# The later modulation's loads moved from SP's queue to GpSimd's, with five tiles instead of three in the second half

## The chip, the cores and the metric

The kernel runs on one core of a Trainium2 chip. The metric is the device time of one execution in microseconds (us). TensorE (PE) multiplies matrices, VectorE (DVE) and ScalarE (ACT) work element by element, GpSimd (POOL) does little here, and SyncE (SP) issues nearly all transfers (DMAs). Each engine works its own instructions off in order and waits for others through semaphores. A DMA is issued by an instruction on some engine's queue, and that instruction may itself wait first.

## What is computed

A decoder trunk of two layers over one sequence of 512 positions and 2048 features, in float32. Layer 0 is differential attention with a SiLU gate, layer 1 forgetting attention over keys and values that are projected once between the two. Ahead of each layer the input is modulated by vectors that come from a condition `c`:

```python
c_act = silu(c)                                   # one row of 2048
for l in range(2):
    shift, scale, gate = split(c_act @ w_mod[l] + b_mod[l], 3)
    h = x * (1 + scale) + shift
    if l == 0:
        y = diff_attention(h, a_w_in, a_w_out, ...)
    else:
        kshift, kscale = split(c_act @ kv_w_mod + kv_b_mod, 2)
        k, v, F = shared_kv(x * (1 + kscale) + kshift, kv_w, kv_b_f)
        y = forgetting_attention(h, b_w_in, b_w_out, k, v, F)
    x = layer_norm(ALPHA * x + gate * y)
```

The products `c_act @ w_mod[l]` and `c_act @ kv_w_mod` are one row times a matrix. Those matrices are large all the same: `w_mod` has 2 x 2048 x 6144 elements and `kv_w_mod` 2048 x 4096.

## The kernel before

**The big products.** Each float32 operand is split into a high part, rounded to the `fp32r` form, and a low part, and a product is three matmuls (`products`, lines 173 to 175). Weights come in steps of 256 rows by 512 columns (`WeightStream`): SP loads a step into a tile `wst` (line 46, four tiles), ScalarE rounds it to `whi` (line 93) and VectorE subtracts to get `wlo` (line 94), three tiles of each. One step feeds 24 matmuls of 512 columns. `group` runs eight such steps for 512 output columns; after every sixth of a step's matmuls (a burst of six) it calls `tick`, which runs one queued piece (attention, for instance) and, where `bg` says so, one step of the background.

**The background: the later modulation.** The shift and scale of layer 0 are made at the start, in another way (`sms`, line 449). All later modulation rows are made by `mod_stream` on VectorE, beside the big products. A segment is 512 columns of one such row: sixteen tiles of 128 rows by 512 columns are multiplied by the matching elements of `c_act` and added into one tile `macc` (line 384 the first of a segment, line 386 the others). Here each such multiply-add is called just that. The summed tile is then split (`mhi`, `mlo`), summed over partitions by two matmuls with a matrix of ones (lines 406 and 407), the bias row `mrow` (loaded at line 403) is added at line 408, and the row goes to DRAM (line 409, tensors `mod_dram` and `gate_dram`), where a later step reads it. There is one `mrow`, so the next bias load waits for the row before to be stored.

There are two such streams.

- The first runs during layer 0: 16 segments, tiles `ms` of two row blocks (512 KB, two multiply-adds), two tiles, one load ahead.
- The second runs during the shared keys and values: 8 segments, tiles `ms` of one row block (256 KB, one multiply-add), three tiles, two loads ahead. The forget gate's rows (`head_rows`) share these tiles.

A load of `ms` (line 369) is issued on SP's queue and waits until the multiply-adds that used the tile are done.

**What sets the order.** The program is written in the order of the big products with `tick` between. A scheduler then fixes each engine's order when the kernel is built, by its own estimate of times: a multiply-add depends on no matmul, so it may be put well ahead of the place where `tick` asks for it, as far as its tiles allow. VectorE's order of multiply-adds and `wlo` subtractions is thus decided when the kernel is built, and at run time a multiply-add whose tile hasn't landed holds up everything behind it on VectorE.

**Attention.** In the first stream's time VectorE also normalises attention outputs (`og`, line 753), which TensorE transposes soon after (line 767).

Of the kernel before, what the change touches and what calls it, by code (L numbers as in the profile page):

```python
# [9 lines left out]
F32 = mybir.dt.float32  # L10
# [5 lines left out]
P = 128  # L16
# [93 lines left out]
def tile_yoco(  # L110
# [23 lines left out]
    nc = tc.nc  # L134
    V, S, PE, G = nc.vector, nc.scalar, nc.tensor, nc.gpsimd
# [25 lines left out]
    def tr_bank(name="tr"):  # L161
        return ps.tile([P, 512], F32, name=name, tag="tr", bufs=1)

    def o_bank(name="o"):
        return ps.tile([P, 512], F32, name=name, tag="o", bufs=1)

    def split(hi, lo, src):
        S.copy(hi, src)
        V.tensor_tensor(lo, src, hi.bitcast(F32), op=ALU.subtract)
# [48 lines left out]
    rows = {}  # L218
# [136 lines left out]
    def mod_stream(segs, new_stage, new_acc, nk):  # L355


        todo = [(i, r) for i in range(len(segs)) for r in range(KT // nk)]
        loaded = {}
        summed = []  # L360

        def load(k):
            if k >= len(todo):
                return
            i, r = todo[k]
            src, col, _ = segs[i]
            t = new_stage()
            rows = src[nk * r * P : nk * (r + 1) * P, col : col + 512]
            nc.sync.dma_start(t, rows.rearrange("(k p) n -> p k n", p=P) if nk > 1 else rows)
            loaded[k] = t  # L370

        ahead = 2 // nk
        for k in range(ahead):
            load(k)
        for k, (i, r) in enumerate(todo):
            load(k + ahead)
            if r == 0:
                acc = new_acc()
            t = loaded.pop(k)
            for kk in range(nk):  # L380
                kt = nk * r + kk
                w = t[:, kk, :] if nk > 1 else t
                if kt == 0:
                    V.tensor_scalar(acc, w, cact[:, 0:1], None, op0=ALU.mult)
                else:
                    V.scalar_tensor_tensor(acc, w, cact[:, kt : kt + 1], acc, op0=ALU.mult, op1=ALU.add)  # L386
                if kt == KT - 1:
                    summed.append(segs[i][2](acc))
                if kt in (1, 5) and summed:
                    if next(summed[0], None) is None:  # L390
                        summed.pop()
                yield
        for _ in summed[0]:
            yield

    def mod_row(pool, ones_r, dst, bias, one):

        def steps(acc):
            hi = pool.tile([P, 512], F32R, name="mhi", tag="mhi", bufs=1)
            lo = pool.tile([P, 512], F32R, name="mlo", tag="mlo", bufs=1)  # L400
            split(hi, lo, acc)
            row = pool.tile([1, 512], F32, name="mrow", tag="mrow", bufs=1)
            nc.sync.dma_start(row, bias.rearrange("(o n) -> o n", o=1))
            yield True
            pt = tr_bank()
            PE.matmul(pt, ones_r, hi, start=True, stop=False)
            PE.matmul(pt, ones_r, lo, start=False, stop=True)
            V.scalar_tensor_tensor(row, pt[0:1, :], one, row, op0=ALU.add, op1=ALU.add)
            nc.sync.dma_start(dst, row)
        return steps  # L410


# [4 lines left out]
    with tc.tile_pool(name="start", bufs=2, reuse_waits="tile") as sp, tc.manual_schedule(engines={ET.DVE}):  # L417
# [64 lines left out]
        ahead = [next(steps)]  # L482
# [147 lines left out]
    for dst, src, col, bias, one in (  # L630
# [5 lines left out]
        for f0 in range(0, D, 512):  # L636
            cs = slice(col + f0, col + f0 + 512)
            segs.append((src, col + f0, mod_row(ap, ones_a, dst[:, f0 : f0 + 512], bias[cs], one)))
    background = mod_stream(
        segs,  # L640
        lambda: ap.tile([P, 2, 512], F32, name="ms", tag="ms", bufs=2),
# [313 lines left out]
    npool, n, nstats = zp  # L955
# [37 lines left out]
    fz = {}  # L993

    def head_rows(tag, bufs):
        return npool.tile([P, T], F32, name="rows", tag=tag, bufs=bufs)[0:B_HEADS, :]

    def forget_logits(q):
        def fn():
            if q == 0:  # L1000
                fz["ps"] = o_bank("zfp")
            for kt in range(4 * q, 4 * q + 4):
                w = zp64[:, kt : kt + 2, :].rearrange("p k n -> p (k n)")
                PE.matmul(fz["ps"], w, Hh[kt], start=kt == 0, stop=False)
                PE.matmul(fz["ps"], w, Hl[kt], start=False, stop=kt == KT - 1)
            if q == 3:
                fz["z"] = head_rows("ms", 3)
                V.tensor_scalar(fz["z"], fz["ps"][0:B_HEADS, :], bf, None, op0=ALU.add)
                V.tensor_tensor(fz["z"], fz["ps"][32 : 32 + B_HEADS, :], fz["z"], op=ALU.add)
        return fn  # L1010

    def forget_sums():

        zf = fz["z"]
        e, w, ln = head_rows("ms", 3), head_rows("ms", 3), head_rows("macc", 2)
        V.scalar_tensor_tensor(e, zf, -1.0, zf, op0=ALU.mult, op1=ALU.max)
        S.activation(e, e, AF.Exp, scale=-1.0)
        V.tensor_scalar(w, e, 1.0, None, op0=ALU.add)
        S.activation(ln, w, AF.Ln)

        V.scalar_tensor_tensor(e, w, -1.0, e, op0=ALU.add, op1=ALU.subtract)
        V.reciprocal(w, w)
        V.tensor_tensor(e, e, w, op=ALU.mult)
        V.tensor_tensor(ln, ln, e, op=ALU.subtract)
        V.scalar_tensor_tensor(zf, zf, 0.0, ln, op0=ALU.min, op1=ALU.subtract)
        V.memset(w, 1.0)
        fz["nf"] = head_rows("macc", 2)
        V.tensor_tensor_scan(fz["nf"], w, zf, 0.0, op0=ALU.mult, op1=ALU.subtract)
        nc.sync.dma_start(f_dram, fz["nf"])
# [29 lines left out]
    for dst, col, one in ((mod_dram[1][1:2, :], D, 1.0), (gate_dram[1], 2 * D, 0.0)):  # L1059
        for f0 in range(0, D, 512):  # L1060
            cs = slice(col + f0, col + f0 + 512)
            segs.append((w_mod[1], col + f0, mod_row(npool, ones_b, dst[:, f0 : f0 + 512], b_mod[1, cs], one)))
    background = mod_stream(
        segs,
        lambda: npool.tile([P, 512], F32, name="ms", tag="ms", bufs=3),
        lambda: npool.tile([P, 512], F32, name="macc", tag="macc", bufs=2),
        1,
    )
# [230 lines left out]
```

## Time and profile before

| What | us |
|---|---|
| Median of 3 runs | 2016.16 (2014.56 to 2017.47) |
| The profiled execution | 2017.03 |
| Its span, from the first to the last instruction | 2015.2 |
| VectorE busy in the span | 1334.4 |
| ScalarE busy in the span | 722.3 |

In the profile's rows, `ms` loads read `in_w_mod_dram` or `in_kv_w_mod_dram`. The first stream's multiply-adds lie between about 186 and 840 us of the span, the second stream's between about 1095 and 1319 us. In a group's row, the number behind `x` is the count, then come the busy time in us and the mean of one in ns, then the idle time just before such instructions and what ended most of it. In a row of waits stand the waiting engine, tile and line, what it waited for, and then the sum in us, how often, and the longest. "SPq" is the time of an issuing instruction on SP.

### The profile page before, as it was taken

The page shows a single profiled execution, that of the slowest core. Times are in us where ns is not written, and L with a number is a line of the kernel's source. Part 1 is how long each engine was busy: PE and PEld are TensorE (multiplying, and loading weights), DVE is VectorE, ACT ScalarE, POOL GpSimd, SP SyncE. Part 2 cuts the span into 40 slices and gives each one's busy share as a digit, 9 for nine tenths or more (in the row PEclk, how much of TensorE's full clock was granted, in tenths as well). Part 3 has the DMA queues.
Part 4 walks back from the last instruction along what each step waited for, and adds up shares of the span by engine and source line. Part 5 has one row for each costly group of instructions (what it writes and reads, how often), then busy time and mean ns, then how long its engine had stood idle before and what let it go on. Part 6 is the DMA issues. An engine that isn't in the chain of part 4 may idle for free.

```text
span 2015.2 us, 25053 instructions
## 1 busy us (share of the span) xinstructions
PE 1966.7 (98%) x9115; PEld 1624.6 (81%) x9115; DVE 1334.4 (66%) x2435; ACT 722.3 (36%) x1230; POOL 2.2 (0%) x10
## 2 busy tenths in 40 slices
PE   5999999999999999999999999999999999999997
PEld 4888878888878888888878877888888888888885
DVE  7887878777667677753575666645455555576678
ACT  2423444433333334432273222224333333453232
POOL 0000000000000000000000000000000000000000
PEclk8999999999999999999999999999999999999998
DMA  9995755574556565552344878844233323333754
GB/s 342 346 314 149 238 174 162 166 222 156 190 166 210 160 225 178 162 165 94 115 144 135 268 252 260 259 123 129 90 104 95 104 90 104 95 117 93 259 191 177
DMA packets 263095, 353.79 MB, mean 176 GB/s; under 512 B 18022, under 2 KB 162556, under 8 KB 262204
## 3 DMA queue, kind: packets, MB, share of 16 engines
q1 hardware_dynamic: 260592, 347.99, 53.7%
q10 hardware_dynamic: 2380, 4.21, 0.6%
q8 instruction: 71, 1.16, 0.2%
q14 instruction: 52, 0.43, 0.1%
HBM read 339.47 MB, written 12.66 MB: 175 GB/s over the span
## 4 chain that ended last, share of the span: by engine, by line
PE 77%; DVE 10%; DMA 10%; issue 2%; ACT 1%; SPq 1%; DVEq 0%; ACTq 0%
PE acc L173 22%; PE acc L175 22%; PE acc L174 22%; DMA ms<-in_w_mod_dram 7%; DVE macc L386 3%; DVE wlo L94 2%; PE sc L173 2%; PE sc L174 2%; PE sc L175 1%; DMA ms<-in_kv_w_mod_dram 1%; PE o L175 1%; PE o L174 1%; PE o L173 1%; PE tr L1163 1%; DMA sms<-in_w_mod_dram 1%
## 5 line engine op out<-in xcount | busy, mean ns | idle before, releaser
L93 ACT CAST whi<-wst 128x1024 fp32r<-128x1024 f32 (+2 forms) x339 | 349.5, 1032 | 672.9 <-PE acc L175 281.6
L94 DVE TENSOR_TENSOR wlo<-wst,whi 128x1024 fp32r<-128x1024 f32 (+2 forms) x339 | 404.4, 1195 | 268.1 <-ACT whi L93 263.9
L173 PE MATMUL acc<-whi,hh 128*128 128x512 f32 x1252 | 492.6, 397 | 0.9 <-ACT hh L933 0.8
L174 PE MATMUL acc<-wlo,hh 128*128 128x512 f32 x1252 | 489.7, 391 | 2.6 <-DVE wlo L94 2.6
L175 PE MATMUL acc<-whi,hl 128*128 128x512 f32 x1252 | 488.1, 390 | 0.0
L173 PE MATMUL acc<-hh,whi 128*128 128x512 f32 x1184 | 468.5, 396 | 1.3 <-ACT vt L977 0.9
L175 PE MATMUL acc<-hh,wlo 128*128 128x512 f32 x1184 | 462.3, 390 | 2.0 <-DVE wlo L94 2.0
L174 PE MATMUL acc<-hl,whi 128*128 128x512 f32 x1184 | 461.7, 390 | 0.0
L386 DVE SCALAR_TENSOR_TENSOR macc<-ms,cact,macc 128x512 f32<-128x512 f32 x360 | 269.9, 750 | 128.4 <-DMA ms<-in_w_mod_dram 95.6
L175 PEld LDWEIGHTS acc<-whi,hl 128*128 128x128 f32 x1252 | 235.3, 188 | 50.8 <-DVE hl L934 0.3
L174 PEld LDWEIGHTS acc<-wlo,hh 128*128 128x128 f32 x1252 | 235.6, 188 | 47.8 <-DVE wlo L94 4.3
L173 PEld LDWEIGHTS acc<-whi,hh 128*128 128x128 f32 x1252 | 235.7, 188 | 46.8 <-ACT hh L933 1.2
L175 PEld LDWEIGHTS acc<-hh,wlo 128*128 128x128 f32 x1184 | 222.3, 188 | 52.2 <-DVE wlo L94 4.2
L173 PEld LDWEIGHTS acc<-hh,whi 128*128 128x128 f32 x1184 | 222.5, 188 | 45.7 <-ACT vt L977 1.7
L174 PEld LDWEIGHTS acc<-hl,whi 128*128 128x128 f32 x1184 | 222.6, 188 | 41.1
L476 DVE SCALAR_TENSOR_TENSOR sacc<-sms,cact,sacc 128x512 f32<-128x512 f32 (+1 forms) x127 | 89.5, 705 | 4.8 <-DMA sms<-in_w_mod_dram 1.2
L1152 ACT ACTIVATE eb<-eb,mnb 128x128 f32<-128x128 f32 (+1 forms) x64 | 36.1, 563 | 96.4 <-DVE mnb L1149 95.2
L703 ACT ACTIVATE e<-e,mn 128x128 f32<-128x128 f32 (+3 forms) x64 | 36.0, 563 | 89.5 <-DVE mn L699 88.7
L1149 DVE CUSTOM_DVE_ANT_0 eb<-sc,biasb 128x128 f32<-128x128 f32 (+1 forms) x64 | 31.3, 490 | 52.7 <-PE sc L175 52.7
L1167 DVE TENSOR_TENSOR pTl<-tr,pTh 128x128 fp32r<-128x128 f32 (+1 forms) x64 | 31.2, 487 | 26.5 <-ACT pTh L1166 26.2
L1166 ACT CAST pTh<-tr 128x128 fp32r<-128x128 f32 (+1 forms) x64 | 27.2, 424 | 43.6 <-PE tr L1163 43.1
L769 ACT ACTIVATE ogT<-tr,subg 128x128 f32<-128x128 f32 x64 | 20.0, 364 | 56.4 <-PE tr L767 56.4
(251 smaller groups left out, 1739.2 us busy)
## 6 DMA issues: line engine op xcount, KB each, us to landing
wst<-in_a_w_in_dram SPq DMA_DIRECT2D x240, 256.0 KB
ms<-in_w_mod_dram SPq DMA_DIRECT2D x64, 512.0 KB
ms<-in_kv_w_mod_dram SPq DMA_DIRECT2D x64, 512.0 KB
wst<-in_kv_w_dram SPq DMA_DIRECT2D x64, 512.0 KB
ms<-in_w_mod_dram SPq DMA_DIRECT2D x128, 256.0 KB
wst<-in_b_w_in_dram SPq DMA_DIRECT2D x128, 256.0 KB
sms<-in_w_mod_dram SPq DMA_DIRECT2D x56, 512.0 KB
wst<-in_b_w_out_dram SPq DMA_DIRECT2D x48, 512.0 KB
```

The lines of the kernel that those rows point to most:

```text
L93: self.nc.scalar.copy(hi[:, :, :w], st[:, :, :w])
L94: self.nc.vector.tensor_tensor(lo[:, :, :w], st[:, :, :w], hi[:, :, :w].bitcast(F32), op=ALU.subtract)
L173: PE.matmul(dst, lhs[0], rhs[0], start=start, stop=False)
L174: PE.matmul(dst, lhs[0], rhs[1], start=False, stop=False)
L175: PE.matmul(dst, lhs[1], rhs[0], start=False, stop=stop)
L386: V.scalar_tensor_tensor(acc, w, cact[:, kt : kt + 1], acc, op0=ALU.mult, op1=ALU.add)
L476: V.scalar_tensor_tensor(acc, w, sc, acc, op0=ALU.mult, op1=ALU.add)
L703: S.activation(e[:, :w], e[:, :w], AF.Exp, bias=mn, scale=-1.0, accum_out=rs)
L1149: V.tensor_tensor_reduce(out=e[:, :w], in0=sc[:, :w], in1=bias[:, :w], scale=-1.0, scalar=3.0e38, op0=ALU.add, op1=ALU.min, accum_out=mn)
L1152: S.activation(e[:, :w], e[:, :w], AF.Exp, bias=mn, scale=-1.0, accum_out=rs)
L1166: S.copy(pTh[:, 0 : i + 1, ts], src)
L1167: V.tensor_tensor(pTl[:, 0 : i + 1, ts], src, pTh[:, 0 : i + 1, ts].bitcast(F32), op=ALU.subtract)
```

## The change

Three edits:

- The loads of `ms`, the bias loads and the stores of finished rows (lines 369, 403, 409) are issued on GpSimd's queue instead of SP's. This holds for both streams.
- The second stream has five `ms` tiles instead of three, and loads four ahead instead of two. The first stream keeps two tiles and one ahead.
- The forget gate's rows, which share the second stream's tiles, ask for the same five.

```diff
             rows = src[nk * r * P : nk * (r + 1) * P, col : col + 512]
-            nc.sync.dma_start(t, rows.rearrange("(k p) n -> p k n", p=P) if nk > 1 else rows)
+            G.dma_start(t, rows.rearrange("(k p) n -> p k n", p=P) if nk > 1 else rows)
             loaded[k] = t

-        ahead = 2 // nk
+        ahead = 4 if nk == 1 else 1
...
             row = pool.tile([1, 512], F32, name="mrow", tag="mrow", bufs=1)
-            nc.sync.dma_start(row, bias.rearrange("(o n) -> o n", o=1))
+            G.dma_start(row, bias.rearrange("(o n) -> o n", o=1))
...
-            nc.sync.dma_start(dst, row)
+            G.dma_start(dst, row)
...
-                fz["z"] = head_rows("ms", 3)
+                fz["z"] = head_rows("ms", 5)
...
-        e, w, ln = head_rows("ms", 3), head_rows("ms", 3), head_rows("macc", 2)
+        e, w, ln = head_rows("ms", 5), head_rows("ms", 5), head_rows("macc", 2)
...
-        lambda: npool.tile([P, 512], F32, name="ms", tag="ms", bufs=3),
+        lambda: npool.tile([P, 512], F32, name="ms", tag="ms", bufs=5),
```

The change also moves instructions. Two places show it. The first is VectorE where the second stream begins, in the second value group of the shared keys and values; `L1028` is the end of the forget gate, `x4` means four in a row. Before:

```order
L1028 SCALAR_TENSOR_TENSOR rows<-rows 16x512
L384 TENSOR_SCALAR macc<-ms,cact 128x512
L1035 TENSOR_SCALAR F<-tr 128x64
L94 TENSOR_TENSOR wlo<-wst,whi 128x1024
L386 SCALAR_TENSOR_TENSOR macc<-ms,cact,macc 128x512 x4
L94 TENSOR_TENSOR wlo<-wst,whi 128x1024
L386 SCALAR_TENSOR_TENSOR macc<-ms,cact,macc 128x512 x3
L94 TENSOR_TENSOR wlo<-wst,whi 128x1024
L386 SCALAR_TENSOR_TENSOR macc<-ms,cact,macc 128x512 x4
L94 TENSOR_TENSOR wlo<-wst,whi 128x1024
```

The same place of VectorE's order now:

```order
L1028 SCALAR_TENSOR_TENSOR rows<-rows 16x512
L384 TENSOR_SCALAR macc<-ms,cact 128x512
L386 SCALAR_TENSOR_TENSOR macc<-ms,cact,macc 128x512
L1035 TENSOR_SCALAR F<-tr 128x64
L386 SCALAR_TENSOR_TENSOR macc<-ms,cact,macc 128x512 x2
L94 TENSOR_TENSOR wlo<-wst,whi 128x1024
L386 SCALAR_TENSOR_TENSOR macc<-ms,cact,macc 128x512 x6
L94 TENSOR_TENSOR wlo<-wst,whi 128x1024
L386 SCALAR_TENSOR_TENSOR macc<-ms,cact,macc 128x512 x5
L94 TENSOR_TENSOR wlo<-wst,whi 128x1024
```

Where three or four multiply-adds stood between two `wlo`, five to seven stand now. The first ten steps behind this place's first `wlo` hold 58 multiply-adds instead of 35; from the twelfth step on, bursts of sixteen in three steps take turns with three or four steps that hold none. Over the whole stream the number is the same, 128.

The second place is SP's queue at the same point of the program (`L1029` stores the forget gate's sums), before:

```order
L46 DMA wst<-in_kv_w_dram 128x2x512
L1029 DMA f_dram<-rows 16x512
L369 DMA ms<-in_w_mod_dram 128x512 x3
L46 DMA wst<-in_kv_w_dram 128x2x512
L369 DMA ms<-in_w_mod_dram 128x512 x4
L46 DMA wst<-in_kv_w_dram 128x2x512
```

And now, on SP:

```order
L46 DMA wst<-in_kv_w_dram 128x2x512 x11
L1029 DMA f_dram<-rows 16x512
L46 DMA wst<-in_kv_w_dram 128x2x512 x25
L898 DMA mrow_b<-mod_dram_76 32x128
L46 DMA wst<-in_kv_w_dram 128x2x512 x21
```

And the start of the second stream on GpSimd, which has nothing else to do there:

```order
L403 DMA mrow<-in_b_mod_dram 1x16x32
L369 DMA ms<-in_w_mod_dram 128x512 x43
L409 DMA mod_dram_76<-mrow 16x1x32
L369 DMA ms<-in_w_mod_dram 128x512
L403 DMA mrow<-in_b_mod_dram 1x16x32
L369 DMA ms<-in_w_mod_dram 128x512 x25
```

SP is left with the weights, and the modulation's loads, bias rows and stores follow one another on GpSimd in the order of the stream.

## The prediction

> **What bounds the kernel now.** I read the busy shares and slices first, then the chain's shares.
>
> ```profile
> PE 1966.7 (98%) x9115; PEld 1624.6 (81%) x9115; DVE 1334.4 (66%) x2435; ACT 722.3 (36%) x1230; POOL 2.2 (0%) x10
> ...
> PE   5999999999999999999999999999999999999997
> ...
> PEclk8999999999999999999999999999999999999998
> DMA  9995755574556565552344878844233323333754
> ...
> PE 77%; DVE 10%; DMA 10%; issue 2%; ACT 1%; SPq 1%; DVEq 0%; ACTq 0%
> ```
>
> TensorE sets the time, at a full granted clock from slice 2 on, and GpSimd stands idle. The windows then say how much TensorE loses, and where (columns: window and its length, busy time and instructions of each engine, clock, DMA share, GB/s).
>
> ```profile
> 0.00:50.00 50.00, 29.04 (x129) 23.42 (x130) 35.51 (x65) 11.78 (x15) 1.60 (x9) 0.90 1.02 342
> 186.00:840.00 654.00, 647.47 (x3050) 536.61 (x3048) 477.11 (x988) 253.77 (x512) 0.00 (x0) 1.00 0.60 188
> 900.00:1000.00 100.00, 100.00 (x443) 82.84 (x442) 42.27 (x61) 20.65 (x22) 0.00 (x0) 1.00 0.33 103
> 1095.00:1319.00 224.00, 218.81 (x954) 177.25 (x953) 144.36 (x182) 55.91 (x66) 0.00 (x0) 1.00 0.78 253
> 2000.00:2016.00 16.00, 1.54 (x7) 0.94 (x5) 11.23 (x22) 0.00 (x0) 0.00 (x0) 0.65 0.32 131
> ```
>
> The first and last rows hold idle time that the change can't reach. The changed loads run in the second row (256 multiply-adds, first modulation stream) and the fourth (128, second stream). From 900 to 1000 us, 443 matmuls pass in 100 us, so one per 0.2257 us. At that pace the fourth window had room for 992 matmuls and holds 954: 38 are missing, **8.6 us lost**. In the second window 654.0 - 647.5 = **6.5 us** are idle. So 15 us is the most that better loads can give back. What TensorE waited for there, the second stream's window first, then the first's:
>
> ```profile
> PE acc L174 <- DVE wlo L94: 2.3, 3, 1.0
> PE acc L175 <- DVE wlo L94: 2.0, 4, 0.9
> ```
> ```profile
> PE tr L767 <- DVE og L753: 4.4, 5, 1.3
> ```
>
> Both are VectorE results that come late. And what VectorE waited for, the second stream's window first:
>
> ```profile
> DVE macc L386 <- DMA ms<-in_w_mod_dram: 72.5, 49, 3.6
> ```
> ```profile
> DVE wlo L94 <- ACT whi L93: 56.9, 36, 4.2
> DVE macc L386 <- DMA ms<-in_kv_w_mod_dram: 26.8, 27, 2.9
> DVE macc L386 <- DMA ms<-in_w_mod_dram: 23.1, 23, 3.1
> DVE macc L384 <- DMA ms<-in_w_mod_dram: 3.1, 2, 2.0
> ```
>
> VectorE works in order: a multiply-add that waits for its `ms` tile holds up the `wlo` (or `og`) behind it. What counts is how long a load takes from a tile's release to its landing, and how the order mixes the two kinds of work.
>
> **The change, part by part.**
>
> *SP relieved.* 256 loads and 48 small transfers leave SP's queue. That is worth nothing by itself: ScalarE, which takes the weights first, waits for TensorE to free its buffers in the second stream (first row), and in the whole first stream only 4.9 us for weights (second).
>
> ```profile
> ACT whi L93 <- PE acc L174: 49.4, 14, 5.6
> ```
> ```profile
> ACT whi L93 <- DMA wst<-in_a_w_in_dram: 4.9, 2, 4.4
> ```
>
> *The second stream, before.* From the `wlo` at 1099.70 to that at 1247.83 VectorE makes 24 weight steps. The grouped rows count what lies between.
>
> ```profile
> 1099.70 1.22 DVE L94 TENSOR_TENSOR wlo<-wst,whi 128x1024 fp32r<-128x1024 f32 x1 [2.49 <-ACT whi L93]
> ...
> 1247.83 1.22 DVE L94 TENSOR_TENSOR wlo<-wst,whi 128x1024 fp32r<-128x1024 f32 x1
> ```
> ```profile
> L386 DVE SCALAR_TENSOR_TENSOR macc<-ms,cact,macc 128x512 f32<-128x512 f32 x80 | 60.0, 751 | 54.6 <-DMA ms<-in_w_mod_dram 53.3
> L94 DVE TENSOR_TENSOR wlo<-wst,whi 128x1024 fp32r<-128x1024 f32 x25 | 30.4, 1217 | 2.5 <-ACT whi L93 2.5
> ...
> L384 DVE TENSOR_SCALAR macc<-ms,cact 128x512 f32<-128x512 f32 x5 | 2.4, 482 | 0.2 <-DMA ms<-in_w_mod_dram 0.2
> ```
>
> TensorE needs 24 matmuls, 5.42 us, per step: 130.1 us. VectorE took 148.1, so it fell 18.0 us behind. TensorE lost 8.6 of that; the other **9.4 us** were its lead (three `whi`/`wlo` buffers). The 85 multiply-adds went at 148.1/85 = 1.74 us each. The load time comes from the chain of waits, which has 23 `ms` rows between 1096 and 1262 us: the shortest, one near the middle, and the longest.
>
> ```profile
> 1155.96 3.99 DMA ms<-in_w_mod_dram
> ...
> 1232.13 2.82 DMA ms<-in_w_mod_dram
> ...
> 1120.66 6.13 DMA ms<-in_w_mod_dram
> ```
>
> The chain follows what came last, so I take 4.0 for a typical load L, just under the middle of 4.35. Three tiles go round in L plus one multiply-add: (4.0 + 0.75)/3 = 1.58 us. The remaining 0.16 is what `wlo` and the other small work add.
>
> *The second stream, after.* Five tiles alone make it (4.75 + d)/5 + 0.16 = 1.11 + 0.2d us per multiply-add, where d is what the new queue and the fuller pipe add to L. But the order has also changed, and that is the trap: the rows now put 58 multiply-adds into the ten steps after the first `wlo` instead of 35. TensorE gives ten steps 54.2 us plus 9.4 of lead, 63.6. VectorE needs 58 x (1.11 + 0.2d) = 64.4 + 11.6d. The loss is 0.8 + 11.6d in place of 8.6: a **net of -7.8 + 11.6d**. Later bursts of 16 in three steps stand behind three or four bare steps, and five tiles are ready, so they cost nothing up to about d = 2. One bias transfer now waits ahead of loads on GpSimd in the dense stretch, for the previous row's store to land: up to one load time, hidden by four tiles in hand. The forget gate's rows share the five tiles, so two loads can start before those rows are done; that is worth one wait at the stretch's start, and I count nothing.
>
> *What d is.* The trace has no load issued from GpSimd. From below: a load from the emptier queue might land as the fastest row did, d = 2.82 - 4.0 = -1.2. From above: the slowest row, d = 6.13 - 4.0 = +2.1. I take **d = 1.0**: two more tiles in flight are 0.52 MB, 1.5 us at the 342 GB/s of the first window, and with the DMA engines 0.78 busy most of that queues. This is nearer to the upper row, and it asks nothing yet of GpSimd's own work. Net: +3.8 us.
>
> The Trainium skill, page "DMA: Bandwidth & Descriptors", section "Latency and other measured facts", gives the first byte as about 0.6 us after an issue from SP and 1 us from GpSimd, where software writes the descriptors. By that alone d = 0.4 and my sum would come to about -0.8 us, 2016; no run here shows it yet.
>
> *How fast GpSimd issues.* At 1.11 us per multiply-add a load must be issued every 1.11 us. On SP a load held the queue this long (minimum, median, maximum in ns):
>
> ```profile
> L369 SPq DMA_DIRECT2D ms<-in_w_mod_dram x127: 327/328/1771, 1096.4 to 1311.4; - x127
> ```
>
> Bounds 0.33 and 1.77 us. I take a value below 1.1, nearer the median, so the issue is hidden; at 1.77 it would not be (below).
>
> *The first stream.* It keeps two tiles, and its VectorE order is moved by a place here and there (in a few places TensorE's transposes of `og` stand one to four matmuls later, under 1 us each, which I leave out). Each of 16 segments is a burst of eight tiles, two in flight, so three round trips wait: a burst ends 3d later, 48d in all. VectorE's waits for these loads are now 26.8 + 23.1 + 3.1 = 53.0 us while TensorE loses 6.5, a ratio of 0.12. So 48 x 0.12 = **5.9d**. The bounds are 0 (the lead of 9.4 and the 56.9 us in which `wlo` waits for ScalarE cover 3 us per burst) and 48 (every burst ends in an `og` that TensorE wants at once). I take 5.9, nearer the low end, since only 4.4 us of `og` waits are seen today.
>
> **Sum:** -7.8 + 17.5d = +9.7 us at d = 1.0. On the profiled execution's 2017.03 (span 2015.2 and 1.8 around it; 0.9 above the median of 2016.16) that is 2026.7, and 2026 as a time to expect beside the median.
>
> **The rivals.** All start from -7.8 + 17.5d.
>
> - *The loads keep pace* (d under 0.2). Speaking for it: SP's queue no longer puts 512 KB of weights ahead of a tile. Then the dense stretch just fits in TensorE's lead and the 8.6 us come back: d = 0 gives 2009. It decides at d = 0.45, where the sum crosses zero. Against it: the DMA share rises.
> - *The two cancel* (d 0.2 to 0.7): the second stream gains what the first loses, within 4 us, so 2013 to 2021. In this case the change does what it says on SP, and the time doesn't show it.
> - *GpSimd is the bound.* If one issue takes 1.77 us, 58 take 102.7, 39.1 beyond the 63.6: +30.5 in the second stream. With d = 1.4 (1.77 less SP's 0.37 for a first-stream load) the first stream adds 8.3: 2056. It decides from 1.11 us per issue on.
> - *VectorE holds GpSimd off.* If an issue must wait for a running VectorE instruction, a multiply-add (0.75) or a `wlo` (1.22), that is about 1 us on top of d = 1.0: d = 2 gives 2044. For it: VectorE is 64% busy in the fourth window. Against it: nothing shows today that the two meet.
>
> The Trainium skill, page "SBUF — State Buffer", section "Who interferes with whom", speaks against the change here: a VectorE instruction in a two-port mode locks GpSimd out, and a DMA issued from GpSimd waits for its descriptors. The multiply-adds have two tensor inputs, and that section counts such an instruction as in the way of GpSimd's reads alone; by it only the quick `L384` (0.48 us for the same 128x512) and the attention's scalings would hold a load up, so it would move few of the 128 loads.
>
> **How the numbers follow.** A measurement of this kernel can tell about 0.2%, 4 us, from no change. Forecast, d 0.7 to 1.5 (2021 to 2035): 0.33. Loads keep pace: 0.19. They cancel: 0.20. GpSimd is the bound: 0.18. VectorE holds it off: 0.10. So faster 0.19, same 0.20, slower 0.33 + 0.18 + 0.10 = 0.61. The range leaves out the best of the first rival and the worst of the third: 2010 to 2058; the forecast's own is 2021 to 2035.
>
> **What would show it.** Right: in the ten steps after the first `wlo` of the second stream VectorE takes 75 us or more and TensorE's waits for `wlo` sit there, while from the twelfth step on they are gone; the chain's `ms` rows are near 5 us; first-stream bursts end about 3 us later and the `og` waits grow. If loads follow each other on GpSimd without a wait for VectorE and more than 1.1 us apart, the third rival holds. Wrong: TensorE's matmul count between 1095 and 1319 reaches 980 or more, or `ms` loads land in 4.2 us or less.

## The result, and the profile after

| | before | after |
|---|---|---|
| Median, us | 2016.82 (2014.56 to 2021.31, 4 runs) | 2036.74 (2031.55 to 2040.32, 4 runs) |
| Profiled execution, us | 2017.03 | 2036.92 |
| Its span, us | 2015.2 | 2035.1 |

The ratio is 1.0094, with a 95% interval of 1.0066 to 1.0122. The change costs 19.9 us; 9.7 were predicted.

The windows of the profile after, over the first stream, the second stream, and the second stream cut at 1200 us (columns as in the prediction):

```profile
186.00:840.00 654.00, 638.51 (x2986) 527.83 (x2985) 463.75 (x963) 247.22 (x500) 102.18 (x148) 0.99 0.58 183
1095.00:1319.00 224.00, 216.73 (x944) 177.23 (x943) 153.25 (x190) 55.89 (x64) 72.69 (x136) 0.99 0.75 252
1095.00:1200.00 105.00, 97.73 (x419) 78.74 (x418) 80.55 (x102) 26.45 (x31) 37.43 (x70) 0.98 0.79 267
1200.00:1319.00 119.00, 119.00 (x526) 98.49 (x526) 72.71 (x89) 29.43 (x33) 35.26 (x66) 1.00 0.71 238
```

In the first stream TensorE is idle for 654 - 638.5 = 15.5 us, before 6.5. In the second it holds 944 matmuls, before 954, and the whole loss is now ahead of 1200 us. TensorE's waits in the two streams follow, and then VectorE's waits for loads in the first:

```profile
PE sc L173 <- DVE mn L699: 3.4, 1, 3.4
PE tr L767 <- DVE og L753: 3.3, 4, 1.4
PE tr L720 <- DVE ss L750: 2.3, 2, 1.3
PE acc L173 <- DVE k1l L169: 2.3, 2, 1.4
```
```profile
PE acc L174 <- DVE wlo L94: 7.3, 5, 2.7
```
```profile
DVE macc L386 <- DMA ms<-in_kv_w_mod_dram: 40.7, 32, 2.8
DVE macc L386 <- DMA ms<-in_w_mod_dram: 35.8, 31, 3.3
DVE macc L384 <- DMA ms<-in_w_mod_dram: 1.3, 1, 1.3
```

VectorE waits 77.8 us for first-stream loads, before 53.0. No single late result takes the time: attention's row maxima (`mn`), sums of squares (`ss`), split keys (`k1l`) and outputs (`og`) are all late at times, each behind multiply-adds in VectorE's order.

How long a GpSimd issue takes (minimum, median, maximum in ns):

```profile
L369 POOL DMA_DIRECT2D ms<-in_w_mod_dram x192: 536/538/877, 164.7 to 1305.6; - x192
L369 POOL DMA_DIRECT2D ms<-in_kv_w_mod_dram x64: 722/722/779, 325.2 to 674.3; - x64
```

0.54 us for 256 KB and 0.72 us for 512 KB. The release of a tile and the next load, on VectorE and then on the issuing queue, before and after:

```profile
226.38 1.54 DVE L386 SCALAR_TENSOR_TENSOR macc<-ms,cact,macc 128x512 f32<-128x512 f32 x2
227.95 0.37 SPq L369 DMA_DIRECT2D ms<-in_w_mod_dram  x1
```
```profile
225.61 1.53 DVE L386 SCALAR_TENSOR_TENSOR macc<-ms,cact,macc 128x512 f32<-128x512 f32 x2
227.45 0.72 POOL L369 DMA_DIRECT2D ms<-in_w_mod_dram  x1 [2.46 <-DVE macc L386]
```

SP follows the last multiply-add by 227.95 - 227.92 = 0.03 us, GpSimd by 227.45 - 227.14 = 0.31. Over all loads of the first stream the trace gives a mean of 0.06 and 0.33 us, and a mean time from issue to landing, by the loads' semaphores, of 4.42 and 4.66 us. So **d is 0.27 + 0.24 = 0.51 us in the first stream**. The 0.24 is GpSimd's longer issue (0.72 us against 0.37) and not a slower transfer: from the end of the issuing instruction a load takes 4.05 us on SP's queue and 3.94 on GpSimd's. In the second stream the mean landing goes from 3.93 to 4.53 us and the issue is 0.26 later in the median: **d is 0.9**.

### The profile page after: what moved, and what is told of

It is laid out like the page before. It is cut to its first block, busy times and chain, and to the rows that moved or that the text cites. A ratio compares the mean times of both kernels' runs of the same rounds, so it can differ in the third digit from the quotient of the medians.

```text
span 2035.1 us, 25176 instructions
## 1 busy us (share of the span) xinstructions
PE 1973.7 (97%) x9115; PEld 1629.4 (80%) x9115; DVE 1335.3 (66%) x2435; ACT 721.5 (35%) x1230; POOL 188.6 (9%) x314
## 3 DMA queue, kind: packets, MB, share of 16 engines
q0 software_dynamic: 30208, 100.78, 15.5%
## 4 chain that ended last, share of the span: by engine, by line
PE 75%; DVE 9%; DMA 9%; issue 5%; POOL 1%; ACT 1%; SPq 1%; DVEq 0%; POOLq 0%; ACTq 0%
PE acc L173 22%; PE acc L175 22%; PE acc L174 22%; DMA ms<-in_w_mod_dram 5%; DMA ms<-in_kv_w_mod_dram 2%; DVE wlo L94 2%; DVE macc L386 2%; DMA sms<-in_w_mod_dram 1%; PE sc L174 1%; PE sc L175 1%; PE sc L173 1%; PE o L175 1%; PE o L173 1%; PE o L174 1%; PE tr L1163 1%
## 5 line engine op out<-in xcount | busy, mean ns | idle before, releaser
L369 POOL DMA_DIRECT2D ms<-in_w_mod_dram x192 | 115.4, 602 | 486.9 <-DVE macc L386 225.9
L369 POOL DMA_DIRECT2D ms<-in_kv_w_mod_dram x64 | 46.6, 728 | 160.7 <-DVE macc L386 119.3
```

The costliest lines, as they stand in the source:

```text
L369: G.dma_start(t, rows.rearrange("(k p) n -> p k n", p=P) if nk > 1 else rows)
```

## The experiments

Ratios are to before, run beside each kernel on the same chip, with 95% intervals. The before's medians were 2017.87, 2018.07 and 2017.54 us in the three groups.

### One stream, or one edit, at a time

`first_pool`: of the change only the first stream's queue (in it, `mod_row` gets its queue as an argument).

```diff
-            nc.sync.dma_start(t, rows.rearrange("(k p) n -> p k n", p=P) if nk > 1 else rows)
+            (G if nk > 1 else nc.sync).dma_start(t, rows.rearrange("(k p) n -> p k n", p=P) if nk > 1 else rows)
...
-            nc.sync.dma_start(row, bias.rearrange("(o n) -> o n", o=1))
+            q.dma_start(row, bias.rearrange("(o n) -> o n", o=1))
...
-            nc.sync.dma_start(dst, row)
+            q.dma_start(dst, row)
```

> Only the first stream's loads and small transfers go to GpSimd's queue; the second stream is that of before (SP's queue, three tiles). Theory A, the first stream was mis-sized: matched by the number of the weight step, the changed kernel falls 14.8 us further behind between 186 and 1095 us, and this comes from the first stream alone. Then this kernel takes 2029 to 2034 us, and TensorE's busy time between 186 and 840 us stays near 638.5 us of 654. Theory B, the prediction's term of 5.9 us per us of added load time holds (with the 0.5 us that the trace of the changed kernel shows between a tile's release and its landing, 3 us; with 1.0, 6 us), and the rest of the changed kernel's loss has another origin: 2019 to 2023 us, busy time near 645 us.

`second_pool`: the second stream alone, GpSimd's queue and five tiles.

```diff
+            (nc.sync if nk > 1 else G).dma_start(t, rows.rearrange("(k p) n -> p k n", p=P) if nk > 1 else rows)
...
+        ahead = 4 if nk == 1 else 1
...
+        lambda: npool.tile([P, 512], F32, name="ms", tag="ms", bufs=5),
```

> Only the second stream has GpSimd's queue and five tiles; the first is that of before. Theory A: the second stream's net is small, +2 us by the weight steps, so 2016 to 2021 us, with VectorE slow in the first ten steps (75 us or more) and TensorE missing nothing after the twelfth. Theory B: the loss sits in the second stream, which then costs 10 us or more beyond the window of 1095 to 1319 us: 2027 or above.

`tiles_only`: before with `ahead = 4` and `bufs=5` in the second stream, all on SP's queue.

> All transfers stay on SP's queue; the second stream has five tiles with four loads ahead. The scheduler puts 45 multiply-adds into the first ten steps of the second stream (before 33, changed kernel 56). Theory A, five tiles are enough if the load time stays near 4 us: 45 multiply-adds of 1.11 to 1.3 us are below TensorE's 63.6 us, so the 8.6 us lost before come back: 2006 to 2011 us. Theory B, on one queue with the weights the fuller pipe lengthens each load (to 6 us or more) and the gain is lost: 2014 to 2019 us.

`queue_only`: all three transfers on `G`, with before's `ahead = 2 // nk` and `bufs=3`.

> All transfers of both streams go to GpSimd's queue, but the second stream keeps three tiles, two ahead. The scheduler's order has 96 multiply-adds in its first 24 steps (before 82), for which TensorE gives 139.5 us with its lead. Theory A: three tiles need (4.75 + d)/3 + 0.16 us per multiply-add, with d 0.3 to 0.9 about 1.84 to 2.04 us, so 177 to 196 us: the second stream loses 37 to 56 us in place of 8.6, and with 15 us of the first stream the time is 2060 to 2080 us. Theory B, the queue costs little in the second stream (d near zero, 1.74 us per multiply-add): 27.5 us lost in place of 8.6, 2040 to 2055 us in all with the first stream.

| | us | ratio |
|---|---|---|
| `first_pool` | 2032.25 | 1.0070 (1.0057 to 1.0083) |
| `second_pool` | 2022.01 | 1.0019 (1.0010 to 1.0028) |
| `tiles_only` | 2010.14 | 0.9960 (0.9947 to 0.9972) |
| `queue_only` | 2063.30 | 1.0226 (1.0212 to 1.0240) |

The first-stream window of `first_pool`:

```profile
186.00:840.00 654.00, 636.96 (x2976) 525.77 (x2975) 461.98 (x960) 245.89 (x498) 101.87 (x148) 0.99 0.58 183
```

The first stream costs 14.4 us by itself, with TensorE 17 us idle, and the second 4.1 (a little above its expected 2016 to 2021). Together 18.5, close to the change's 19.9, and theory A in both. Five tiles on SP's queue gain 7.7 us, close to the 8.6 that the second stream lost. Three tiles on GpSimd's queue are far worse: 31 us more than `first_pool`, within theory A's range. How much of it is the queue's is open, for this kernel was not run in another order: with the expectation's figures (27.5 us lost at 1.74 us per multiply-add, in place of 8.6) 18.9 of the 31 us would come from its order alone, by estimate.

### The queue, or the order that came with it

Moving the loads also made the scheduler write another order. To part the two, all instructions of VectorE, TensorE and ScalarE were held to the order of another kernel by order-only edges (dependencies that fix what comes first when the kernel is built); the rows of the three engines then stand exactly as in that kernel, while the queue stays. The four kernels below differ from those above only by this, the lists of instruction names left out here:

```diff
+def pin(tc, order):
+    seen = {i.name: i for i in tc.nc.all_instructions()}
+    kind = mybir.DependencyInfo(mybir.DependencyClass.NoSync, mybir.DependencyReason.DATA)
...
+        for a, b in zip(names, names[1:]):
+            tc.add_manual_dep(seen[b], a, kind, reason="order")
...
         tile_yoco(tc, *args)
+        pin(tc, ORDER)
```

`first_pool_pin` is `first_pool` in before's order:

> The first stream on GpSimd's queue, the second as before, and VectorE, TensorE and ScalarE held to before's order of instructions by order-only edges. The same kernel in its own order took 14.4 us more than before (2032.25 against 2017.87). Theory A, the loss is in the loads: each tile is 0.5 us later (0.27 from release to issue, 0.24 to 0.27 in the load), VectorE's waits for the loads grow by 20 us or more, and TensorE has no slack left for that: 2028 to 2034 us. Theory B, the loss is in the scheduler's new order of some rows (score steps and root-mean-square steps behind multiply-adds): 2016 to 2022 us.

`first_sp_pin` is before in `first_pool`'s order:

> The reverse: every transfer on SP's queue as before, but VectorE, TensorE and ScalarE held to the order that the scheduler made for the first stream on GpSimd's queue. Theory A (the loads): 2015 to 2021 us, as before. Theory B (the order): 2028 to 2034 us. A time between says that both have a part, and how large.

`second_pool_pin` is `second_pool` in the order of `tiles_only`:

> The second stream on GpSimd's queue with five tiles, the first as before, and the three engines held to the order made for five tiles on SP's queue: 45 multiply-adds in the first ten steps instead of 56. In its own dense order this kernel took 2022.0 us, and five tiles on SP's queue 2010.1. Theory A, the dense order costs the difference: the loads land in 4.6 us here and in 4.8 us there, so 2008 to 2013 us. Theory B, the queue costs it (issue after release 0.3 us later, 0.54 us of GpSimd per load): 2018 to 2024 us.

`second_sp_pin` is `tiles_only` in the order of `second_pool`:

> The reverse: five tiles on SP's queue, but the three engines held to the dense order made for GpSimd's queue (56 multiply-adds in the first ten steps). Theory A (the order): 2019 to 2024 us, with TensorE losing 10 us or more in the first twelve steps. Theory B (the queue): 2008 to 2013 us, as with five tiles on SP's queue in their own order.

| | SP's queue | GpSimd's queue |
|---|---|---|
| first stream, before's order | 2018.07 | 2031.08, ratio 1.0062 (1.0046 to 1.0077) |
| first stream, new order | 2023.15, ratio 1.0026 (1.0018 to 1.0035) | 2032.25 (above) |
| second stream, 46 multiply-adds in ten steps | 2010.14 (above) | 2010.53, ratio 0.9963 (0.9950 to 0.9975) |
| second stream, 58 in ten steps | 2021.24, ratio 1.0018 (1.0010 to 1.0027) | 2022.01 (above) |

(46 and 58 are counted as in the prediction, between the first `wlo` and the eleventh; the expectations count the ten groups that begin one step earlier: 45, where the trace has 44, and 56.)

**The second stream is all order.** In either order the two queues are within 0.8 us; between the orders lie 11 us. The second-stream windows, sparse order on GpSimd's queue, then dense order on SP's:

```profile
1095.00:1319.00 224.00, 224.00 (x990) 184.75 (x988) 151.88 (x192) 58.32 (x68) 73.72 (x138) 1.00 0.75 259
```
```profile
1095.00:1319.00 224.00, 213.73 (x930) 174.40 (x929) 146.28 (x183) 55.60 (x66) 0.00 (x0) 0.99 0.77 254
1095.00:1200.00 105.00, 94.73 (x405) 75.99 (x404) 75.90 (x99) 24.00 (x28) 0.00 (x0) 0.98 0.86 289
```

With 46, TensorE is never idle, though its loads come through GpSimd. With 58 on SP's queue it loses 10.3 us before 1200. Nor is the longer load time the queue's: the mean landing is 4.75 us in the first of these and 4.58 in the second, against 4.80 in `tiles_only`; three tiles in flight had 3.93 (on GpSimd's queue, in `queue_only`, 3.79). It comes with the five tiles.

**The first stream is mostly the loads.** In before's order they cost 13.0 us. The order alone costs 5.1, and both together 14.4, so they overlap. As the expectation had it, a time between says that both have a part. One place where the order costs, in VectorE's rows of before and then of `first_sp_pin`:

```profile
226.38 1.54 DVE L386 SCALAR_TENSOR_TENSOR macc<-ms,cact,macc 128x512 f32<-128x512 f32 x2
229.30 0.75 DVE L386 SCALAR_TENSOR_TENSOR macc<-ms,cact,macc 128x512 f32<-128x512 f32 x1 [1.38 <-DMA ms<-in_w_mod_dram]
229.97 0.28 DVE L699 CUSTOM_DVE_ANT_0 e<-sc,bias 128x128 f32<-128x128 f32 x1
```
```profile
232.14 1.54 DVE L386 SCALAR_TENSOR_TENSOR macc<-ms,cact,macc 128x512 f32<-128x512 f32 x2 [1.71 <-DMA ms<-in_w_mod_dram]
236.07 1.54 DVE L386 SCALAR_TENSOR_TENSOR macc<-ms,cact,macc 128x512 f32<-128x512 f32 x2 [2.39 <-DMA ms<-in_w_mod_dram]
237.52 0.28 DVE L699 CUSTOM_DVE_ANT_0 e<-sc,bias 128x128 f32<-128x128 f32 x1
```

After `neglam` (L239) three multiply-adds stood ahead of the score row that gives `mn`; now four do. From the first of them to the score row it takes 3.6 us before and 5.4 here, and TensorE waits 2.7 us at that place, by its view of waits:

```profile
PE sc L173 <- DVE mn L699: 2.7, 1, 2.7
```

### How TensorE's loss follows VectorE's waits

`loads_first_pin` takes the small transfers back to SP's queue (before's order):

> Of the first stream only the 128 loads of 512 KB go to GpSimd's queue; its bias rows and stores stay on SP's queue, the second stream is as before, and VectorE, TensorE and ScalarE are held to before's order. With the small transfers on GpSimd too this took 2031.1 us, 13.0 more than before. Theory A, the loads alone cost it (each tile 0.5 us later from release to landing): 2028 to 2034 us. Theory B, the stores at the head of GpSimd's queue, which wait up to 31 us for their row, hold loads up: 2016 to 2024 us without them.

`first_halves_pin` brings each 512 KB tile by two loads on GpSimd's queue (before's order):

```diff
+            if nk > 1:
+                for h in range(nk):
+                    G.dma_start(t[:, h, :], rows[h * P : (h + 1) * P, :])
```

> The first stream on GpSimd's queue in before's order, as above with its small transfers, but each tile of 512 KB is brought by two loads of 256 KB one behind the other. GpSimd then spends 2 x 0.54 us per tile instead of 0.72, so the second half starts 0.4 to 0.8 us later and the tile is full some 0.4 us later. Theory A, the cost follows the time from release to landing (13.0 us for 0.51): 0.9 us give about 23 us, 2036 to 2046 us. Theory B, the cost comes from the queue being another and not from its time: 2028 to 2034 us. If the halves land no later, or earlier, A asks for 2031 us or less, in proportion to the time measured.

`best1`: everything on SP's queue, finer tiles in the first stream.

```diff
+        first = len(segs) > 8
...
+        ahead = 3 if first else 4
...
-        lambda: ap.tile([P, 2, 512], F32, name="ms", tag="ms", bufs=2),
+        lambda: ap.tile([P, 512], F32, name="ms", tag="ms", bufs=4),
...
-        2,
+        1,
```

> All on SP's queue; five tiles of 256 KB in the second stream, and in the first four tiles of 256 KB with three loads ahead in place of two of 512 KB with one ahead (the same bytes of SBUF). Theory A, the first stream's loss is load time that two tiles don't hide: four tiles need (4.4 + 0.75)/4 = 1.3 us per multiply-add, two of 512 KB (4.4 + 1.5)/4 = 1.5 us, so VectorE's waits for loads in the first stream shrink from 53 us to 30 to 40, and part of the 6.5 us idle there comes back: 2003 to 2009 us. Theory B, the denser order that the scheduler makes of it costs what is gained: 2010 to 2016 us.

`fine_pool_pin`: the same with all transfers on `G`, held to the order of `best1`.

> The same tiles as the run before (four of 256 KB in the first stream, five in the second), all loads and small transfers of both streams on GpSimd's queue, and the three engines held to the order made for SP's queue. Theory A, a queue that delivers 0.5 us later costs (4.4 + 0.75 + 0.5)/4 - 1.29 = 0.12 us per multiply-add in the first stream, 256 x 0.12 = 31 us of VectorE's waits at most, of which the 16 bursts hide what stands before them: 5 to 15 us above the run before. Theory B, with more loads in flight the later landing is hidden as in the second stream, where it cost nothing with five tiles: within 4 us of the run before.

The first-stream windows and VectorE's waits for loads in them, of `first_pool_pin`, `loads_first_pin` and `first_halves_pin`:

```profile
186.00:840.00 654.00, 637.12 (x2971) 525.11 (x2970) 461.72 (x960) 244.95 (x497) 101.48 (x147) 0.99 0.58 183
DVE macc L386 <- DMA ms<-in_kv_w_mod_dram: 45.1, 29, 3.2
DVE macc L386 <- DMA ms<-in_w_mod_dram: 30.3, 25, 2.8
DVE macc L384 <- DMA ms<-in_w_mod_dram: 2.6, 2, 1.5
```
```profile
186.00:840.00 654.00, 640.44 (x2997) 528.79 (x2996) 466.25 (x965) 249.76 (x504) 88.87 (x123) 1.00 0.59 185
DVE macc L386 <- DMA ms<-in_kv_w_mod_dram: 39.8, 31, 2.5
DVE macc L386 <- DMA ms<-in_w_mod_dram: 30.9, 25, 2.8
DVE macc L384 <- DMA ms<-in_w_mod_dram: 2.8, 2, 1.4
```
```profile
186.00:840.00 654.00, 652.41 (x3075) 541.27 (x3074) 480.43 (x1001) 256.40 (x518) 147.13 (x277) 1.00 0.58 189
DVE macc L390 <- DMA ms<-in_kv_w_mod_dram: 20.9, 26, 1.6
DVE macc L390 <- DMA ms<-in_w_mod_dram: 19.2, 20, 3.4
```

| before's order, first stream | VectorE's waits for loads | TensorE idle | time | ratio |
|---|---|---|---|---|
| `first_halves_pin` | 40.1 | 1.6 | 2012.39 | 0.9976 (0.9966 to 0.9986) |
| before | 53.0 | 6.5 | 2017.54 | |
| `loads_first_pin` | 73.5 | 13.6 | 2026.87 | 1.0054 (1.0040 to 1.0067) |
| `first_pool_pin` | 78.0 | 16.9 | 2031.08 | 1.0062 (1.0046 to 1.0077) |

One order, four load times: TensorE's idle time rises with VectorE's waits by (16.9 - 6.5)/(78.0 - 53.0) = 0.42, (13.6 - 6.5)/20.5 = 0.35 and (6.5 - 1.6)/12.9 = 0.38 us per us. The halves were expected to be later and came earlier: their multiply-adds wait less, and the time falls below before's although everything still goes through GpSimd. This speaks for the load time and against the queue as such. `loads_first_pin` came out between its two ranges, nearer theory A's; whether the small transfers cost the remaining 4 us the overlapping intervals don't say.

The waits and idle times are those of the profiled executions, which took 2010.99, 2017.03, 2024.96 and 2034.34 us in the table's order, and not of the medians. By these times a us of waiting, more or less than before's, was worth 0.47, 0.39 and 0.69 us. The slope is thus known only roughly, as 0.4 to 0.7.

Now `best1` (2012.41, ratio 0.9982, 0.9973 to 0.9990) and `fine_pool_pin` (2015.02, ratio 0.9984, 0.9975 to 0.9993). The first-stream window of each:

```profile
186.00:840.00 654.00, 646.71 (x3032) 534.98 (x3031) 474.62 (x983) 250.57 (x506) 0.00 (x0) 1.00 0.58 187
```
```profile
186.00:840.00 654.00, 644.20 (x3021) 532.84 (x3020) 472.11 (x978) 250.78 (x505) 146.91 (x275) 1.00 0.57 187
```

`best1` falls to theory B: VectorE's waits shrank to 38.6 us, but TensorE is idle for 7.3 us, not less than before (the profiled execution took 2015.19 us, 2.8 more than the median). The order that the scheduler made of four tiles is the likely cause; `best1` in another order was not tried. `fine_pool_pin` lies 2.6 us above it by the medians and 0.4 by the ratios, within theory B's 4: with four finer tiles GpSimd's later issue is nearly hidden.

The fastest is `tiles_only`, 2010.14 us, 0.4% below before, with `second_pool_pin` (2010.53) level. Halved loads in the first stream with five tiles in the second were not run together, nor halves on SP's queue.

## Why the prediction was right in its sign, and where it was off

*The second stream: right.* Its term was -7.8 + 11.6d; at the measured d = 0.9 that is +2.6, at the predicted 1.0 it is +3.8, and alone it measured +4.1. Ten steps were to take 75 us or more; they take 1189.81 - 1116.79 = 73.0, a little less:

```profile
1116.79 1.22 DVE L94 TENSOR_TENSOR wlo<-wst,whi 128x1024 fp32r<-128x1024 f32 x1
...
1189.81 1.22 DVE L94 TENSOR_TENSOR wlo<-wst,whi 128x1024 fp32r<-128x1024 f32 x1
```

That is 1.26 us for each of the 58 multiply-adds (predicted 1.31). TensorE's waits for `wlo` sit there and are gone after it. The reason for d, two more tiles in flight, holds too: SP's queue shows the same landing with five tiles. The gain and the dense order are both real, -8 and +11 us.

*SP relieved, GpSimd's issues, VectorE's hold.* That SP's relief is worth nothing by itself fits the runs: in one order the kernel takes the same time with the second stream on either queue (2010.14 and 2010.53 us). An issue takes 0.54 us, so GpSimd is no bound at 1.26 us per multiply-add: the third rival falls. The fourth, a hold of about 1 us, falls by the steady 0.3 us from release to issue. The store that waits at the head of GpSimd's queue was not among the rivals, and the trace shows no first-stream load that it held: the three latest were issued 1.06 to 1.92 us after their tile came free, and each 3.1 us or more after the last store or bias load was issued. In the second stream five loads near 1202 us came 4.0 to 5.5 us late. Ahead of them the bias load had waited 4.05 us for the row's store to land, which is the hold that the prediction named; it fell behind the dense stretch, where TensorE lost nothing.

*The first stream: the step that failed.* "I take 5.9, nearer the low end": the 48d behind it was right, since in before's order VectorE's waits grew by 78.0 - 53.0 = 25.0 us, and 48 x 0.51 is 24.5. In the profile after, a burst takes 27.2 us on average, before 25.6; 3d is 1.5. The ratio was wrong. The prediction divided TensorE's idle time by VectorE's waits, 6.5/53.0 = 0.12, an average over waits of which most were already hidden; an added wait costs 0.35 to 0.42 us of idle time, and 13.0/25.0 = 0.52 us of the kernel's (0.4 to 0.7, as above). At d = 0.51 the term gave 3.0 us, and the loads measured 13.0. The smaller error is in the same part: the order's moves "under 1 us each, which I leave out" cost 5.1 us alone and, by the medians, 1.4 on top of the loads.

So the total came nearer than its parts, by luck: at the measured d they give 5.6 us, and the 1.0 taken for the first stream, twice the measured value, made up some of the missing ratio. The time of 2036.74 lies inside the range, and 1.7 us beyond the forecast's own 2035. The `og` waits, which were to grow, did not in the changed kernel (4.4 to 3.3 us); `mn`, `ss` and `k1l` took their place. In before's order they did grow (`first_pool_pin`, 5.4 us), so which result is late is a matter of the order.

On the page "DMA: Bandwidth & Descriptors", section "Latency and other measured facts", the Trainium skill's 0.4 us more from GpSimd than from SP to the first byte lies between the first stream's 0.24 from issue to landing and the 0.51 with the later issue. By that figure and the measured ratio the first stream would lose 48 x 0.4 x 0.52 = 10 us, an estimate.

## What to carry to other kernels

The average of "TensorE idle per us of VectorE waiting" says nothing about the next us of waiting: count how much hidden time is left behind each wait, or test it with one slower load. When a change alters tiles or queues under a scheduler, hold the engines' order fixed once with order-only edges and run queue and order apart; here the same five tiles on the same queue gain 8 us or lose 3 by the order alone. Where few tiles are in flight, two half loads that each release their own work can be worth more than another queue: here they took 2031.1 us to 2012.4 with queue and order unchanged.

## What the runs showed of the hardware

**The first of two half loads lands well ahead of the whole.** From the pages' list of DMA issues, KB each and median us to landing, of `first_pool_pin` and `first_halves_pin`:

```profile
ms<-in_w_mod_dram POOLq DMA_DIRECT2D x64, 512.0 KB, 4.7
ms<-in_kv_w_mod_dram POOLq DMA_DIRECT2D x64, 512.0 KB, 4.5
```
```profile
ms<-in_w_mod_dram POOLq DMA_DIRECT2D x128, 256.0 KB, 3.9
ms<-in_kv_w_mod_dram POOLq DMA_DIRECT2D x128, 256.0 KB, 3.6
```

The first multiply-add needs only the first half, which by these medians is there 0.8 to 0.9 us sooner than the whole tile. By the tiles' means, from the first issue on, the first half is there after 3.70 us and the second after 4.56, against 4.71 for the whole: the second comes 0.86 us behind the first, about when the first multiply-add of 0.75 us ends. By the fit on the page "DMA: Bandwidth & Descriptors", section "Anatomy of one DMA — SWDGE (gpsimd) path", the Trainium skill's figures give an estimate of 0.6 us for the 256 KB saved, which is near.

**The granted clock fell after every stall of 2.65 us or more, and after some shorter ones.** Windows of the profile after, where TensorE waited 3.4 us for `mn`; of `queue_only`, where it waited 2.1 us at the same place; and of `loads_first_pin`, where it waited 2.1 us for `sg`:

```profile
230.00:235.00 5.00, 3.00 (x15) 2.18 (x13) 1.86 (x3) 0.61 (x1) 0.72 (x1) 1.00 0.77 256
235.00:240.00 5.00, 3.56 (x10) 2.98 (x11) 4.96 (x15) 1.16 (x5) 1.24 (x2) 0.54 0.53 161
240.00:245.00 5.00, 5.00 (x22) 4.17 (x21) 3.85 (x12) 2.25 (x6) 0.93 (x2) 0.78 0.71 219
```
```profile
230.00:235.00 5.00, 2.94 (x16) 2.12 (x14) 3.28 (x7) 0.57 (x2) 0.72 (x1) 1.00 0.82 263
235.00:240.00 5.00, 4.30 (x21) 3.42 (x22) 3.69 (x11) 1.56 (x6) 1.44 (x2) 1.00 0.85 269
```
```profile
793.00:796.00 3.00, 0.89 (x5) 0.45 (x4) 2.41 (x6) 0.38 (x1) 0.36 (x1) 0.97 0.63 206
796.00:799.00 3.00, 3.00 (x8) 2.32 (x9) 2.55 (x3) 0.00 (x0) 0.48 (x2) 0.50 0.57 175
```

Over all the traces, between 100 and 1990 us, seven stalls of TensorE lasted 2.65 to 3.46 us, and after each the clock fell to 0.50, for 3.4 or 6.8 us. Of the sixteen that lasted 1.84 to 2.32 us it fell after seven, and after none that was shorter; what decides between them no run here shows. The fall at 235 us seems to have cost little: `first_pool` and `queue_only`, which share the first stream's order, reach the same `wlo` at the same time, one with the fall and one without:

```profile
275.08 1.22 DVE L94 TENSOR_TENSOR wlo<-wst,whi 128x1024 fp32r<-128x1024 f32 x1
```
```profile
275.10 1.22 DVE L94 TENSOR_TENSOR wlo<-wst,whi 128x1024 fp32r<-128x1024 f32 x1
```

Between 230 and 275 us TensorE stood idle for 3.8 us in `first_pool` and 5.4 in `queue_only`, so what the one spent at the lower clock the other spent waiting for VectorE. No run was made for the clock alone.
